# A hybrid decoder layer: DeltaNet rows in two buffers, mixer work moved between VectorE, GpSimd and ScalarE, and new task orders

## The chip, the cores and the metric

The kernel runs on one core of a Trainium2 chip. The metric is device time in microseconds of one launch. A core has TensorE (PE in the profile, its weight loads PEld), VectorE (DVE), ScalarE (ACT), GpSimd (POOL) and SyncE (SP), which here only issues DMAs; each engine works through its own queue in order.

## What is computed

One layer with 512 tokens of width 1024, float32 throughout:

```python
h = swiglu(rms_norm(x, g1), w_gate, w_up, w_down)            # width 2816
x = x + 0.5 * rms_norm(h, g1_post)
u = rms_norm(x, g_mix)                                        # u @ w_in feeds three mixers:
o_nsa = g0*compressed_attn + g1*selected_attn + g2*window_attn   # 8 heads of 64, T5 bias
dq, dk, dv = split(silu(causal_conv4(dn_qkv)))                # gated DeltaNet, 4 heads of 128
o_dn  = rms_norm(gated_delta_rule(l2(dq), l2(dk), dv, log_decay, beta), g) * silu(z)
o_mem = cross_attention(mem_q, rms_norm(mem))                 # 4 heads of 128, 256 memory tokens
merged = sum(sigmoid(u @ w_branch_gate)[b] * (o_b @ w_branch[b]) for b in (nsa, dn, mem))
x = x + rms_norm(merged @ w_out, g_post)
x = x + 0.5 * rms_norm(swiglu(rms_norm(x, g2), ...), g2_post)
```

The delta rule in its chunked form solves, for each head and chunk, a unit lower triangular system whose matrix is `beta_i * (k_i . k_j) * exp(gc_i - gc_j)` below the diagonal, `gc` being the running sum of the log decay.

## The kernel before

Float32 products are made of three products of split operands (`mm3`, L115, with the lines L117, L118, L119 of the profile): a weight block is loaded (`wraw`), cast on ScalarE (`whi`, L106) and its remainder taken on VectorE or, for a chosen share, on GpSimd (`wlo`, L109). A projection of the mixer is 24 such products of 128x512. A `wraw` buffer can be loaded again only when the remainder has been taken, and all weight loads go through SP's queue.

The launch is one long program, unrolled. In order: the first layer's first tiles (from 0 us), the rest of the first FFN as Strassen-like products of seven (L489, to about 232), its down product and norms (to about 365), the mixer's projections and the DeltaNet (365 to 600), the sparse attention (600 to 760), memory attention and the gated merge (760 to 900), the output product and norm (to about 980), and the second FFN.

What runs inside a stage is cut into tasks, a letter with digits, and lists in the dictionary `PRM` give their order (`tasks`, L1413). The order is a priority: a scheduler at build time takes the ready instruction of the highest priority for each engine, so tasks interleave. `off` gives a task a lead of so many places; `pool` says which share of its weight remainders goes to GpSimd (0 none, 1 all, 2 every second, 3 every third). On the chip each queue is then fixed.

First layer (`order_s`): `wFIC` loads and splits the weights of tile F, I = 0 gate or 1 up, half C; `t0K` transposes four blocks of the first 256 tokens (`feat`); `P0C`, `P1C` are the half products of tiles 0 and 1 (`half`); `y` and `x` load the rest of the input; `R`, `n` are norms; `F` finish tiles.

Mixer (`order`): `cHS` is projection and causal convolution of head H, part S (0 query, 1 key, 2 value; `dn_conv`, L886). `hHS` (`dn_head`, L905) transposes it, takes the squares on ScalarE (L924), a chain of small VectorE steps for the inverse root (L138 to L148), scales (`kn` or `qs`, L930) and transposes back (L937, `ptk`). `rH` (`dn_rows`, L941) loads two rows of scalars spread over all partitions (`rows`: the running log decay and beta) and makes `eg` and `dec` by exponentials. `lH` (`dn_lt`) makes the triangular matrix from `kbT`, the key transform times beta, and sends it to memory; `kH` (`dn_qk`) makes the query side. For a pair of heads `bI` (`dn_subst`, L987) reads the 16x16 diagonal blocks back and inverts them in 30 small VectorE steps (L1001, L1003, tile `Bi`) and sends them out and in again (`Dc`); `eI` (`dn_double`) expands them into four block diagonal matrices (L1021); `dIK` doubles the inverse block size, `sIN` runs the states over the four chunks and `oI` ends. `i` and `z` are projections with tokens as rows, `a` the scalars of the decay, `x`, `p`, `f` the compressed keys, `q` the attention queries.

Attention (`order2`): `S` are scores and softmax of one head and branch over four query blocks (`nsa_soft`; L1305 bias and minimum on VectorE, L1306 exponential on ScalarE, then scaling by `psc`, one letter for each query block, v VectorE or s ScalarE), `P` transposes and evicts the probabilities (`nsa_pt`, three evictions by `ptc`), `V` and `W` the products with the values, `M` merge tiles. `order4` is the merge with memory attention, `order3` the output product.

Of the kernel before, what the change touches and what calls it, by code (L numbers as in the profile page):

```python
# [10 lines left out]
F32 = mybir.dt.float32  # L11
# [4 lines left out]
OP = mybir.AluOpType  # L16
AX = mybir.AxisListType
P = 128
D = 1024
KT = 8  # L20
TB = 4
# [18 lines left out]
class Body:  # L40
    def __init__(self, ctx, tc, a, out, tap):
        self.tc, self.nc, self.a, self.out, self.tap = tc, tc.nc, a, out, tap
        pool = lambda name, **k: ctx.enter_context(tc.tile_pool(name=name, **k))
        self.sp = pool("sp", bufs=2)
        self.cp = pool("cp", bufs=1)
        self.ring, self.ringi = None, 0
        self.nload, self.pool_every = 0, 0
        self.tp = pool("tp", bufs=2)
        self.wp = pool("wp", bufs=1)
        self.wx, self.nx = None, 0  # L50
        self.ps = pool("ps", bufs=1, space=bass.MemoryType.PSUM)
        self.dr = pool("dr", bufs=1, space=bass.MemoryType.DRAM)
        nc = self.nc
        wm = self.tp.tile([P, 512], BF16, tag="tmpb", bufs=2, name="wm")
        nc.vector.memset(wm, 0.0)
        w1 = self.sp.tile([P, 1], F32, tag="w1", name="w1", bufs=1)
        nc.gpsimd.memset(w1, 0.0)
        nc.scalar.activation(w1, w1, AF.Silu)
        pw = self.bank("o", "warm")
        for _ in range(PRM.get("warm", 10)):  # L60
            nc.tensor.matmul(pw, wm[:, :P], wm, start=True, stop=True)
        self.cst = self.cp.tile([P, C_END], F32, name="cst")
        nc.sync.dma_start(self.cst[:, :P], a["consts"][:, :P])
        x = self.load_x(a["x"], tbs=(0, 1), c=slice(0, 512))
        self.ident = self.cst[:, C_ID : C_ID + P]
        self.gpre = self.sp.tile([P, 4, KT], F32, name="gpre", bufs=1)
        self.msk = self.sp.tile([P, 9], F32, name="msk", bufs=1)
        nc.sync.dma_start(self.gpre, a["gains_pre"])
        self.x0 = x
        self.own = 0  # L70
        self.side = []
# [869 lines left out]
    def dn_rows(self, h, sc, d):  # L941

        nc, g = self.nc, self.nc.gpsimd
        sg, gc, beta, nbg, dr = sc
        rows = self.da.tile([P, 2, TB, P], F32, tag="rows", name="rowsb", bufs=1)
        self.dma("r").dma_start(rows, dr[h].partition_broadcast(P))
        eg = self.da.tile(self.T4, F32, tag="eg", name="eg", bufs=1)
        dec = self.da.tile(self.T4, F32, tag="dec", name="dec", bufs=1)
        nc.scalar.activation(eg, rows[:, 0], AF.Exp)
        g.tensor_tensor(dec, rows[:, 0], gc[:, :, h, None].to_broadcast(self.T4), op=OP.subtract)  # L950
        g.tensor_tensor(dec, dec, self.cst[:, None, C_NEG : C_NEG + P].to_broadcast(self.T4), op=OP.add)
        nc.scalar.activation(dec, dec, AF.Exp)
        d.update(rows=rows, eg=eg, dec=dec)

    def dn_lt(self, h, d, dp):

        nc, v, g, te = self.nc, self.nc.vector, self.nc.gpsimd, self.nc.tensor
        kbT = self.da.tile(self.T4, F32, tag="kbT", name="kbT", bufs=1)
        g.tensor_tensor(kbT, d["kT"], d["rows"][:, 1], op=OP.mult)
        d["LT"] = dp.tile(self.T4, F32, tag="LT", name="LT", bufs=2)  # L960
        self.dn_kk(d["kT"], kbT, d["LT"], d["dec"])
        if h % 2 == 0:
            self.dL = self.dr.tile([2, TB, P * P + P], F32, name=f"dL{h}")
        self.dma("l").dma_start(self.dL[h % 2, :, : P * P].rearrange("n (p i) -> p n i", p=P), d["LT"])
        d["kd"] = dp.tile(self.T4, F32, tag="kd", name="kd", bufs=4)
        g.tensor_tensor(d["kd"], d["k"], d["dec"][:, :, P - 1 : P].to_broadcast(self.T4), op=OP.mult)

    def dn_qk(self, h, d, dp):

        g = self.nc.gpsimd  # L970
        d["qdT"] = dp.tile(self.T4, F32, tag="qdT", name="qdT", bufs=4)
        g.tensor_tensor(d["qdT"], d["qT"], d["eg"], op=OP.mult)
        d["gl"] = dp.tile([P, TB], F32, tag="gl", name="gl", bufs=4)
        g.tensor_copy(d["gl"], d["eg"][:, :, P - 1])
        d["QK"] = dp.tile(self.T4, F32, tag="QK", name="QK", bufs=4)
        self.dn_kk(d["kT"], d["qT"], d["QK"], d["dec"])

    def dn_kk(self, kT, rhs, dst, dec):
        p = self.psb("e", "pkk")
        for n in range(TB):  # L980
            self.nc.tensor.matmul(p[:, n], kT[:, n], rhs[:, n], start=True, stop=True)
        self.nc.vector.tensor_tensor(dst, p, dec, op=OP.mult)

    def dma(self, k):
        return getattr(self.nc, PRM.get("dma", {}).get(k, "sync"))

    def dn_subst(self, h, dp):  # L987

        nc, v, g = self.nc, self.nc.vector, self.nc.gpsimd
# [388 lines left out]
    def merge_tile(self, br, j, uh, ul, oh, ol, mg, first, gate=None, pair=None):  # L1378
        nc, v = self.nc, self.nc.vector
# [515 lines left out]
```

## Time and profile before

| | |
|---|---|
| median of three runs | 1285.19 us (1284.23 to 1287.13) |
| the profiled execution | 1285.44 us |
| its span, first to last instruction | 1283.7 us |
| mean granted TensorE clock | 0.994 |
| busy: TensorE, VectorE, ScalarE, GpSimd | 98%, 77%, 57%, 14% |
| chain that ended last | TensorE 84%, VectorE 8%, DMA 3%, ScalarE 3% |

The profile is one execution. Its page gives busy time by engine, the chain of work that ended last, and groups of instructions; further views give waits, stretches of time and single instructions. A matmul's end is modelled, so a busy TensorE can still run slowly: the granted clock has to be read beside it. A wait is put down to what came last before it ended. An idle engine that is not the bottleneck costs nothing.

### The profile page before, as it was taken

The page shows a single profiled execution, that of the slowest core. Times are in us where ns is not written, and L with a number is a line of the kernel's source. Part 1 is how long each engine was busy: PE and PEld are TensorE (multiplying, and loading weights), DVE is VectorE, ACT ScalarE, POOL GpSimd, SP SyncE. Part 2 cuts the span into 40 slices and gives each one's busy share as a digit, 9 for nine tenths or more (in the row PEclk, how much of TensorE's full clock was granted, in tenths as well). Part 3 has the DMA queues.
Part 4 walks back from the last instruction along what each step waited for, and adds up shares of the span by engine and source line. Part 5 has one row for each costly group of instructions (what it writes and reads, how often), then busy time and mean ns, then how long its engine had stood idle before and what let it go on. Part 6 is the DMA issues. An engine that isn't in the chain of part 4 may idle for free.

```text
span 1283.7 us, 21891 instructions
## 1 busy us (share of the span) xinstructions
PE 1258.7 (98%) x8067; PEld 1103.3 (86%) x8067; DVE 990.8 (77%) x1803; ACT 730.8 (57%) x1487; POOL 182.5 (14%) x208
## 2 busy tenths in 40 slices
PE   8999999999999999999999999999999999999997
PEld 7899999888787778888777778898888999998886
DVE  6897887598967866755789766675797987886888
ACT  6556665685755634415565545444676666655663
POOL 0011111130002221102221110010200121110300
PEclk9999999999999989999999999999999999999999
DMA  6567656894753341233221142131953677664963
GB/s 221 178 203 182 172 172 124 240 215 169 245 187 116 104 109 58 83 111 114 75 59 58 42 141 82 58 106 67 316 185 115 222 172 202 177 125 163 238 213 115
DMA packets 109243, 190.38 MB, mean 148 GB/s; under 512 B 18652, under 2 KB 28240, under 8 KB 109136
## 3 DMA queue, kind: packets, MB, share of 16 engines
q1 hardware_dynamic: 92976, 154.12, 36.5%
q0 software_dynamic: 15872, 34.61, 13.7%
q8 instruction: 63, 1.03, 0.3%
q10 hardware_dynamic: 288, 0.26, 0.1%
q14 instruction: 44, 0.36, 0.1%
HBM read 178.90 MB, written 33.08 MB: 165 GB/s over the span
## 4 chain that ended last, share of the span: by engine, by line
PE 84%; DVE 8%; DMA 3%; ACT 3%; issue 2%; SPq 0%; POOL 0%; DVEq 0%; ACTq 0%
PE smm L489 11%; PE se L489 7%; PE acc_mm L723 7%; PE pfm L117 5%; PE pfm L119 5%; PE pfm L118 5%; PE acc_s L723 4%; PE ss L489 4%; PE so L489 2%; PE sr L489 2%; PE ps L1303 2%; PE de L489 2%; PE po L1339 1%; PE ppt L1325 1%; PE acc_e L723 1%
## 5 line engine op out<-in xcount | busy, mean ns | idle before, releaser
L106 ACT CAST whi<-wraw 128x512 fp32r<-128x512 f32 (+1 forms) x174 | 105.5, 612 | 116.6 <-PE pfm L119 63.0
L109 DVE TENSOR_TENSOR wlo<-wraw,whi 128x512 fp32r<-128x512 f32 (+1 forms) x142 | 95.9, 684 | 36.7 <-ACT whi L106 35.2
L586 POOL DMA_DIRECT2D T<-in_ffn_d_dram x88 | 59.7, 678 | 377.8 <-PE pg L119 110.0
L117 PE MATMUL pfm<-xth,whi 128*128 128x512 f32 x272 | 107.9, 402 | 0.6 <-DVE X L1188 0.3
L118 PE MATMUL pfm<-xth,wlo 128*128 128x512 f32 x272 | 108.3, 403 | 0.0
L119 PE MATMUL pfm<-xtl,whi 128*128 128x512 f32 x272 | 107.8, 402 | 0.0
L489 PE MATMUL smm<-thi,fset 128*128 128x256 f32 x432 | 76.4, 277 | 0.5 <-ACT ss L496 0.5
L109 POOL TENSOR_TENSOR wlo<-wraw,whi 128x512 fp32r<-128x512 f32 x29 | 38.3, 1322 | 267.0 <-ACT whi L106 259.0
L489 PEld LDWEIGHTS smm<-thi,fset 128*128 128x128 f32 x432 | 65.2, 188 | 0.8 <-ACT ss L496 0.7
L117 PEld LDWEIGHTS pfm<-xth,whi 128*128 128x128 f32 x272 | 51.1, 189 | 10.9 <-issue 0.7
L119 PEld LDWEIGHTS pfm<-xtl,whi 128*128 128x128 f32 x272 | 50.9, 188 | 9.2 <-issue 0.4
L118 PEld LDWEIGHTS pfm<-xth,wlo 128*128 128x128 f32 x272 | 50.9, 188 | 8.7
L705 ACT CAST ringh<-ringr 128x1024 fp32r<-128x1024 f32 (+1 forms) x44 | 45.0, 1032 | 23.2 <-PE acc_mm L723 7.6
L489 PE MATMUL smm<-thi,fxth 128*128 128x256 f32 x204 | 56.4, 277 | 0.0
L489 PE MATMUL smm<-thi,fxtl 128*128 128x256 f32 x204 | 56.3, 276 | 0.0
L496 ACT COPY se<-smm 128x256 f32<-128x256 f32 x70 | 25.0, 358 | 53.4 <-PE smm L489 53.4
L489 PE MATMUL se<-thi,fset 128*128 128x256 f32 x288 | 50.8, 276 | 0.0
L738 DVE TENSOR_TENSOR sl<-H,sh 128x1024 fp32r<-128x1024 f32 (+2 forms) x38 | 40.9, 1080 | 5.4 <-ACT sh L737 5.3
L428 DVE TENSOR_TENSOR fs<-fq 128x1024 f32<-128x1024 f32 x35 | 43.3, 1238 | 1.0
L1306 ACT ACTIVATE Pm<-Pm,nm 128x384 f32<-128x384 f32 (+2 forms) x64 | 35.6, 557 | 14.4 <-DVE nm L1305 13.9
L489 PEld LDWEIGHTS se<-thi,fset 128*128 128x128 f32 x288 | 43.4, 188 | 0.0
L737 ACT CAST sh<-H 128x1024 fp32r<-128x1024 f32 (+2 forms) x38 | 35.4, 939 | 12.9 <-DVE H L645 4.1
(652 smaller groups left out, 4353.8 us busy)
## 6 DMA issues: line engine op xcount, KB each, us to landing
T<-in_ffn_d_dram POOLq DMA_DIRECT2D x88, 256.0 KB, 4.1
fq<-in_ffn_g_dram SPq DMA_DIRECT2D x70, 256.0 KB, 3.1
fq<-in_ffn_u_dram SPq DMA_DIRECT2D x70, 256.0 KB, 3.9
wraw<-in_ffn_d_dram SPq DMA_DIRECT2D x34, 256.0 KB, 3.7
ringr<-T SPq DMA_DIRECT2D x16, 512.0 KB, 5.7
ringr<-in_ffn_d_dram POOLq DMA_DIRECT2D x16, 512.0 KB, 8.1
woraw<-in_w_out_dram SPq DMA_DIRECT2D x32, 256.0 KB, 4.0
mfq<-in_w_gate_dram SPq DMA_DIRECT2D x28, 256.0 KB, 2.9
```

The costliest lines, as they stand in the source:

```text
L106: nc.scalar.copy(hi, raw)
L109: self.lmark = eng.tensor_tensor(lo, raw, hi.bitcast(F32), op=OP.subtract)
L117: t.matmul(out, lh, rh, start=first, stop=False)
L118: t.matmul(out, ll, rh, start=False, stop=False)
L119: self.tick(t.matmul(out, lh, rl, start=False, stop=last), 3 * math.prod(out.shape[1:]))
L428: add = lambda *x: v.tensor_tensor(*x, op=OP.add)
L489: m = lambda x, y, **kw: te.matmul(out, x, y, skip_group_check=True, **kw)
L586: i = g.dma_start(o[c], x[c], max_dma_last_dim=2048, **({"accum_op": OP.add} if add else {}))
L705: nc.scalar.copy(hi, raw)
L723: e = lambda a, b, s, f: nc.tensor.matmul(acc[i], a, b, start=s, stop=f, skip_group_check=True)
L738: last = tt(low, f, hi.bitcast(F32), op=OP.subtract)
L1306: nc.scalar.activation(pm, pm, AF.Exp, bias=nm[:, qb : qb + 1], scale=-1.0, accum_out=sm[:, qb : qb + 1])
```

## The change

- `rows` gets two buffers instead of one (another 4 KB of each partition).
- `dec` is made on VectorE in four operations of 128x128 (subtract, then add the mask) instead of two of 128x512 on GpSimd. `kbT` and the small `gl` move from GpSimd to VectorE; `kd` and `qdT` stay on GpSimd.
- The four block expansions of each pair (L1021) all go to GpSimd; three of four were on VectorE (`xpd`).
- Copies and scalings: the convolution's first scaling to ScalarE (`cva`), the scaling of the two narrow query blocks and the second eviction of the transposed probabilities to ScalarE (`psc`, `ptc`), the two copies of the third level swapped (`t1c`).
- In the first layer the gate half of tile 0's first half product goes first (`gu`), `t01` goes before `t00`, and a new task `m8` issues eight dummy products into an otherwise unused bank, the same as the eight at the start.
- New orders, leads and GpSimd shares for the first layer, mixer, attention, merge and output. `gon2` orders the last transposes of a pair behind the last scaled output. `mge` has the value it had.

```diff
-... 'xpd': (0, 1, 2), ... 'ptc': 'vvs', 'cva': 'v', ... 'psc': 'vvvv', ... 't1c': 'vs', ... 'gon2': 0}
+PRM = {'eng': {'rows': 2, 'dec': 's', 'dec2': 'v', 'kbT': 'v', 'kd': 'g', 'qdT': 'g', 'gl': 'v'}, ...
+... 'xpd': (), ... 'ptc': 'vss', 'cva': 's', ... 'psc': 'ssvv', ... 't1c': 'sv', ... 'gon2': 1, 'mge': 'v', 'gu': ((0, 1), (1, 0), (1, 0), (1, 0))}
 order_s (first layer), up to w111
-  w000 t00 w010 t01 P00 w110 y w100 t03 t02 P10 w011 w001 P01 w111
+  w000 t01 w010 t00 m8 w110 y P00 w100 t03 P10 t02 w011 w001 P01 w111
 order (mixer)
-  i a w c01 h01 r0 c00 c10 c02 l0 h00 h02 c11 c12 k0 h10 c22 h12 h11 c21 r1 k1 l1 h21 h22 b0 e0 z c20 r2 h20 c32 l2 c31
-  d00 k2 h31 r3 d01 l3 b1 d02 x0 s00 e1 d10 c30 h32 x1 h30 d11 s01 s02 s03 q3 p0 d12 o0 p1 k3 q0 p2 p3 s10 p4 q1 p5 s11
-  p6 p7 s12 s13 o1 q2 f
+  i a w c01 c10 h01 c00 r0 c02 l0 h00 h02 h10 c11 c12 k0 r1 h12 h11 c21 k1 c22 l1 b0 h21 h22 z c20 c32 e0 r2 h20 r3 c31 l2
+  d00 d01 h31 k2 l3 d02 x0 b1 h32 e1 s00 c30 s01 s02 s03 d10 x1 h30 d11 q3 p0 q0 d12 p1 o0 p2 p3 k3 s10 s11 p4 q1 p5
+  p6 s12 s13 p7 o1 f q2
 off (leads; those that the text names)
-  b0 300, h21 20, h22 100, e0 100
+  b0 100, h21 400, h22 20, e0 20
...
-        rows = self.da.tile([P, 2, TB, P], F32, tag="rows", name="rowsb", bufs=1)
+        rows = self.da.tile([P, 2, TB, P], F32, tag="rows", name="rowsb", bufs=PRM["eng"]["rows"])
...
-        g.tensor_tensor(dec, rows[:, 0], gc[:, :, h, None].to_broadcast(self.T4), op=OP.subtract)
-        g.tensor_tensor(dec, dec, self.cst[:, None, C_NEG : C_NEG + P].to_broadcast(self.T4), op=OP.add)
+        if PRM["eng"]["dec"] == "s":
+            for n in range(TB):
+                nc.vector.scalar_tensor_tensor(dec[:, n], rows[:, 0, n], gc[:, n, h : h + 1], self.cst[:, C_NEG : C_NEG + P], op0=OP.subtract, op1=OP.add)
...
-        g.tensor_tensor(kbT, d["kT"], d["rows"][:, 1], op=OP.mult)
+        self.eng("kbT").tensor_tensor(kbT, d["kT"], d["rows"][:, 1], op=OP.mult)
...
-                for i in (1, 0):
+                for i in PRM["gu"][2 * f + c]:
...
-                "w": weights, "P": half,
+                "w": weights, "P": half, "m": self.warm,
```

The new orders of attention, merge and output move single tasks by a few places: in attention the score task S001 goes behind P000, Q2 and Q3 go later, and the load of the memory keys (L) goes earlier; in the merge A00 goes first and A20 earlier; in the output stage the splits run 3 6 5 7 2 1 4 0 instead of 2 3 7 6 5 1 0 4.

More of the change, by code (lines that the diff above doesn't have):

```diff
@@ L59, in __init__, with warm @@
         pw = self.bank("o", "warm")
-        for _ in range(PRM.get("warm", 10)):
-            nc.tensor.matmul(pw, wm[:, :P], wm, start=True, stop=True)
+        def warm(n):
+            for _ in range(n):
+                nc.tensor.matmul(pw, wm[:, :P], wm, start=True, stop=True)
+        self.warm = warm
+        warm(PRM["warm"])
         self.cst = self.cp.tile([P, C_END], F32, name="cst")
@@ L949, in dn_rows @@
         nc.scalar.activation(eg, rows[:, 0], AF.Exp)
-        g.tensor_tensor(dec, rows[:, 0], gc[:, :, h, None].to_broadcast(self.T4), op=OP.subtract)
-        g.tensor_tensor(dec, dec, self.cst[:, None, C_NEG : C_NEG + P].to_broadcast(self.T4), op=OP.add)
+        if PRM["eng"]["dec"] == "s":
+            for n in range(TB):
+                nc.vector.scalar_tensor_tensor(dec[:, n], rows[:, 0, n], gc[:, n, h : h + 1], self.cst[:, C_NEG : C_NEG + P], op0=OP.subtract, op1=OP.add)
+        else:
+            self.eng("dec").tensor_tensor(dec, rows[:, 0], gc[:, :, h, None].to_broadcast(self.T4), op=OP.subtract)
+            self.eng("dec2").tensor_tensor(dec, dec, self.cst[:, None, C_NEG : C_NEG + P].to_broadcast(self.T4), op=OP.add)
         nc.scalar.activation(dec, dec, AF.Exp)
@@ L965, in dn_lt @@
         d["kd"] = dp.tile(self.T4, F32, tag="kd", name="kd", bufs=4)
-        g.tensor_tensor(d["kd"], d["k"], d["dec"][:, :, P - 1 : P].to_broadcast(self.T4), op=OP.mult)
+        self.eng("kd").tensor_tensor(d["kd"], d["k"], d["dec"][:, :, P - 1 : P].to_broadcast(self.T4), op=OP.mult)
     def dn_qk(self, h, d, dp):
@@ L971, in dn_qk @@
         d["qdT"] = dp.tile(self.T4, F32, tag="qdT", name="qdT", bufs=4)
-        g.tensor_tensor(d["qdT"], d["qT"], d["eg"], op=OP.mult)
+        self.eng("qdT").tensor_tensor(d["qdT"], d["qT"], d["eg"], op=OP.mult)
         d["gl"] = dp.tile([P, TB], F32, tag="gl", name="gl", bufs=4)
-        g.tensor_copy(d["gl"], d["eg"][:, :, P - 1])
+        self.eng("gl").tensor_copy(d["gl"], d["eg"][:, :, P - 1])
         d["QK"] = dp.tile(self.T4, F32, tag="QK", name="QK", bufs=4)
@@ L982, in dn_kk, with eng @@
         self.nc.vector.tensor_tensor(dst, p, dec, op=OP.mult)
+    def eng(self, k):
+        return self.nc.vector if PRM["eng"][k] == "v" else self.nc.gpsimd
     def dma(self, k):
@@ L1387, in merge_tile @@
         v.scalar_tensor_tensor(t2, t, 1.0, pp, op0=OP.add, op1=OP.mult)
-        return v.tensor_tensor(mg[:, j], mg[:, j], t2, op=OP.add)
+        return (nc.vector if PRM["mge"] == "v" else nc.gpsimd).tensor_tensor(mg[:, j], mg[:, j], t2, op=OP.add)
     def token_sums(self, k, uh, ul, tt, hi, lo):
```

2 lines of the change are left out of this document (1 added, 1 removed).

## The prediction

> **What bounds the kernel now.** I read the shares of the engines first, then busy time by stage, then the list of what TensorE waits for, then its clock, and only then single instructions.
>
> ```profile
> PE 1258.7 (98%) x8067; PEld 1103.3 (86%) x8067; DVE 990.8 (77%) x1803; ACT 730.8 (57%) x1487; POOL 182.5 (14%) x208
> ```
> ```profile
> 365.00:480.00 115.00, 107.30 (x564) 90.70 (x565) 80.68 (x198) 60.08 (x134) 22.56 (x23) 0.97 0.40 116
> 605.00:760.00 155.00, 153.95 (x834) 117.02 (x835) 124.94 (x344) 85.84 (x223) 25.70 (x20) 1.00 0.23 74
> 760.00:910.00 150.00, 148.92 (x939) 131.66 (x939) 98.31 (x145) 76.21 (x162) 14.35 (x10) 1.00 0.32 103
> ```
> ```profile
> core 0 of [0], span 1283.7 us
> engine line waited for: us in total, times, longest us
> PE ptk L937 <- DVE Bi L1003: 3.0, 1, 3.0
> PE pu L117 <- ACT k L466: 2.8, 1, 2.8
> PE ptk L937 <- DVE kn L930: 1.7, 1, 1.7
> PE warm L61 <- DVE wm L55: 1.2, 1, 1.2
> PE pfm L117 <- DVE tg L1387: 1.1, 1, 1.1
> PE acc_e L723 <- DVE wlo L109: 0.9, 1, 0.9
> PE ptk L937 <- DVE qs L930: 0.9, 1, 0.9
> PE ppt L1325 <- DVE Pm L229: 0.7, 1, 0.7
> PE pkk L981 <- POOL kbT L959: 0.7, 1, 0.7
> ```
>
> TensorE is busy 1258.7 of 1283.7 us, so 25.0 us of span is all that new orders can win by filling idle time. The columns of the stage rows are length, then busy time of PE, PEld, DVE, ACT and POOL. The mixer's first part (365 to 480) holds 7.7 us of the idle; attention (605 to 760) has 1.05 and the merge (760 to 910) 1.08. The wait list says where: four of the nine longest waits (3.0, 1.7, 0.9, 0.7) are the DeltaNet heads of the mixer, one (2.8) is the first layer. "Busy" hides a second loss, the clock:
>
> ```profile
> 6.33:9.18 2.85, 0.00 (x1) 0.00 (x1) 1.95 (x5) 2.03 (x5) 0.00 (x0) 1.00 0.87 308
> 9.44:12.85 3.41, 3.41 (x18) 3.41 (x18) 2.10 (x4) 1.19 (x3) 0.00 (x0) 0.50 0.74 249
> 456.58:460.00 3.42, 2.47 (x10) 2.40 (x11) 3.39 (x9) 0.49 (x1) 1.47 (x1) 0.50 0.22 69
> 460.00:463.41 3.41, 3.41 (x9) 2.64 (x9) 3.16 (x10) 0.71 (x2) 1.28 (x1) 0.50 0.16 49
> ```
>
> The value after the five engines is the granted clock. After the first layer's empty 2.85 us it is 0.50 for 3.41 us, all of them busy: half of that, 1.7 us, is lost on top of the gap. After the mixer's 3.0 us wait it is 0.50 for 2.47 + 3.41 = 5.88 busy us: 2.9 lost. So the two long waits cost 2.85 + 1.7 and 3.0 + 2.9. On what lowers the clock, the Trainium skill ("TensorE: Matmul & The Clock Gate", Part 1) states that it takes at least one idle window of about 3.4 us. The stretch of 3.41 us agrees; the idle of 2.85 before it does not, and the trace decides; what follows if the page is right stands among the rivals.
>
> **The change part by part.** First layer: the gate half of the first tile goes before the up half, two feature transposes are swapped, and eight dummy products follow them.
>
> ```profile
> 1.20 3.60 PE L61 MATMUL warm<-wm 128*128 128x512 bf16 x8 [1.20 <-DVE wm L55]
> ...
> 7.38 0.69 DVE L467 TENSOR_TENSOR k<-wraw,k 128x512 fp32r<-128x512 f32 x1
> ...
> 8.51 0.62 ACT L466 CAST k<-wraw 128x512 fp32r<-128x512 f32 x1 [0.78 <-DMA wraw<-in_ffn_u_dram]
> ...
> 13.92 0.84 ACT L212 ACTIVATE xth<-ptr,gpre 128x256 fp32r<-128x256 f32 x2 [2.18 <-PE ptr L208]
> ```
>
> The gate weights are split at 7.38 + 0.69 = 8.07, the up weights cast only at 9.13. With gate first TensorE can start 9.18 - 8.07 = 1.1 us sooner, and the dummies fill 6.33 to 8.1 and should keep the clock up: the same eight took 3.60 us before, 0.45 each, which is the pace of half clock (nine wide products in 3.41 us above, 0.38 each), so about 1.8 at full. At half clock they would run to 9.9 and cost 0.75. The most to be had is 2.85 + 1.7 = 4.55, the least a loss of 0.75. What is late next is the transfer of the next weights, whose buffers come free behind ScalarE's evictions; these stood idle 2.18 us for TensorE's transposes, and that is as far as they can move forward. I take -2.2. The dummies add no transfer and wait for nothing new.
>
> Mixer, the wait at 454 us. Its chain is in these rows (waits of SP's queue, waits of ScalarE, then single instructions):
>
> ```profile
> SPq L946 <- POOL kbT L959: 10.7, 3, 7.0
> ```
> ```profile
> ACT L949 <- DMA rowsb<-drows: 1.8, 1, 1.8
> ```
> ```profile
> 453.15 0.28 ACT L924 ACTIVATE sq<-ptr 128x128 bf16<-128x128 f32 x1
> ...
> 455.26 0.17 DVE L1001 TENSOR_TENSOR Bt<-Lb,Bi 64x15 f32<-64x15 f32 x1 [0.80 <-DMA Lb<-dL]
> ...
> 456.69 0.69 DVE L930 TENSOR_TENSOR kn<-ptr,dry 128x512 f32<-128x512 f32 x1
> 457.53 0.45 PE L937 MATMUL ptk<-cst,kn 128*128 128x128 f32 x1 [3.00 <-DVE Bi L1003]
> ```
>
> The one `rows` buffer is read last by kbT on GpSimd, so three of the four row loads held SP's queue, 10.7 us in all with the weight loads behind them. The load then lands late; ScalarE stands 1.8 us on it with a head's squares queued behind (last at 453.15); the head's norm on VectorE therefore meets the substitution, whose first step holds VectorE until its own transfer lands at 455.26; `kn` comes at 456.69 and TensorE has run out. A second buffer lets the row load go a head earlier: the 1.8 us go, the squares end near 451.6, and the small steps of the norm (L138 to L148) are through before the substitution's transfer blocks the queue. The order helps at the same place (the substitution's lead falls from 300 to 100, head 2's key transform gains one, from 20 to 400). I take the whole 3.0 + 2.9 = -5.9; the least is 0, if VectorE's queue still puts the substitution in front. Next in line is the substitution itself, which then starts no later than now.
>
> The 1.7 us wait for the first head's `kn`: one more projection (24 products) is placed ahead of that head. At full clock nine products take half of 3.41 us, so 24 take 4.5 and cover it: -1.7. The 0.9 wait for `qs` is merely moved: half, -0.45.
>
> Engines. The prices:
>
> ```profile
> L1021 DVE TENSOR_TENSOR Dm<-Dc,msk 128x512 f32<-128x512 f32 x4 | 3.8, 998 | 1.7 <-DMA Dc<-dD 1.7
> ...
> L1021 DVE TENSOR_TENSOR DT<-Dc,msk 128x512 f32<-128x512 f32 x2 | 1.4, 678 | 0.0
> ```
> ```profile
> L1021 POOL TENSOR_TENSOR DT<-Dc,msk 128x512 f32<-128x512 f32 x2 | 2.6, 1313 | 7.1 <-PE pfm L118 4.0 <-DMA Dc<-dD 3.2
> ```
> ```profile
> L951 POOL TENSOR_TENSOR dec<-dec,cst 128x512 f32<-128x512 f32 x4 | 5.1, 1283 | 0.3
> ```
> ```profile
> L229 DVE TENSOR_SCALAR cacc<-pfm,cw 128x512 f32<-128x512 f32 x12 | 9.0, 747 | 9.3 <-PE pfm L119 9.3
> ```
> ```profile
> L1306 ACT ACTIVATE Pm<-Pm,nm 128x512 f32<-128x512 f32 x16 | 11.5, 718 | 1.3 <-DVE nm L1305 0.9
> ```
>
> kbT on VectorE: 0.69 (the kn row, same size) for about 1.28, which takes 0.6 off the 0.7 wait: -0.6. Decay: two GpSimd passes of up to 1.28 a head become four VectorE passes over a quarter each; no row has that form, so 4 x 0.17 (the smallest VectorE step above) to 4 x 0.69 bounds them, 0.7 to 2.8 a head; nearer the first, a quarter of 0.69 being 0.17. Four heads of kbT and decay add 4 x (0.69 + 0.7) = 5.6 to VectorE; the conv's scaling to ScalarE takes 9.0 away, and three of the four expansions of each pair another 3.8 + 1.4 = 5.2. VectorE ends lighter by 8.6, behind TensorE and worth nothing by itself. The scaling waits on ScalarE for a projection's last product, as the VectorE row does now (9.3 us idle), and the casts of the next weights stand behind it; ScalarE is busy 60 of 115 us, so I give that nothing of its own.
>
> The expansions: four in a row on GpSimd take 4 x 1.31 = 5.2 us, where VectorE did three and GpSimd one side by side in about 3 x 1.0 = 3.0, so the level products can start 2.2 later per pair, 4.4 in all at worst. They are off the path where TensorE still has projections: from 365 to 480 it is short of operands, not of work. Behind them on GpSimd's queue stand the mask clears of the levels and the weight splits given to it, on whose buffers SP's loads wait. I take +0.5, ends 0 and +4.4. The Trainium skill ("GPSIMD Engine Reference", Specifications) speaks against this part: GpSimd shares its SBUF interfaces with VectorE and collides with its two-input operations. The trace agrees, 998 ns beside GpSimd and 678 without; were the eight VectorE operations beside each pair's expansions all stretched by that 0.32 us on the path, the time would be 5 us more, about 1282.
>
> Attention, merge, output. Scaling of the two narrow probability blocks and one eviction in three of the transposed ones go from VectorE (125 of 155 us busy) to ScalarE (86 of 155), and the orders move some tasks. Against me stand 16 blocks whose scaling now queues on ScalarE, for me the waits 0.7 (Pm) and 1.1 (tg). I take -1.0, ends -1.8 and the slow rival below. The order of the splits in the output stage, the swapped copies at the third level and the new shares of weight splitting on GpSimd I cost at nothing: TensorE's queue covers them, and where it doesn't they are new waits.
>
> New waits: an order that moves every head brings its own. The only row for that is the stretch itself: from 0 to another 7.7 us. I take 3.0, less than half, since VectorE is lighter.
>
> **Sum.** -2.2 - 5.9 - 1.7 - 0.45 - 0.6 + 0.5 - 1.0 + 3.0 = -8.35. The profiled execution took 1285.44 us (span 1283.7 and 1.7 around it), 0.25 above the median of 1285.19; so 1276.8, called 1277.
>
> **The rivals.** (a) The second buffer does not free the wait at 454, because VectorE's queue still holds the substitution in front of `kn`: +5.9, 1282.7. For it: the 0.80 us on the substitution's transfer stays. Against: the norm was late by ScalarE's 1.8 us first. (b) Waits only move: the mixer's new waits equal the old (7.7 of idle instead of 3.0 and the start held by transfers): 1276.8 + 4.7 + 2.2 = 1283.7, and without attention's 1.0, 1284.7. For it: every wait in the list is short and single, which is what a shuffled order leaves. (c) Idle time does not set the clock, so halves come where they came: 1276.8 + 2.9 = 1279.7, called 1280. This is where the clock page's window of 3.4 us would lead. Both half-clock stretches follow the longest waits, which speaks against it. (d) Slower: ScalarE as attention's queue. The scaling of a block there queues behind an exponential of the next (0.72 us), and the transposes wait for it, 16 times: 11.5 us, with attention's gain of 1.0 gone, 1289.3. It decides from about 0.6 us a block, 10 us together. Against: TensorE is full there (153.95 of 155) and has merge products to slip between.
>
> **How the numbers follow.** Forecast 0.60, (a) 0.12, (b) 0.10, (c) 0.04, (d) 0.14. 0.2% is 2.6 us, about what a measurement of this kernel can tell from no change. (a) lies on that edge, half of it to each side: faster 0.60 + 0.04 + 0.06 = 0.70; same 0.06 + 0.10 = 0.16; slower 0.14. The forecast's own range is 1269.5 (start -4.55, qs -0.9, attention -1.8, no new waits, no cost of expansions) to 1282. The range takes in (a), (b), (c) and the foot of (d): 1269 to 1287.
>
> **What would show it.** Right: TensorE's first product on weights near 8 us and no half clock before 13; no row wait of SP on kbT, no ScalarE wait on rowsb, no wait of ptk above 1 us and a clock of 1.00 through 480; the 365 to 480 work over 5 us shorter. Wrong: a new half-clock stretch anywhere, a wait of ppt on ScalarE in attention, pt waiting for GpSimd's expansions, or the start's gain given back to a weight transfer before 35 us.

## The result and the profile after

The changed kernel takes 1301.6 us in the median (1287.5 to 1303.3, 11 runs) against 1284.2 (1283.5 to 1287.1, 11 runs): ratio 1.0101, 95% interval 1.0073 to 1.0128. It is slower by 1%, where 1277 was forecast, with 1269 to 1287 as the range. The number needs one remark: the changed kernel's own times fall in two groups, 1287.5 to 1289.7 (4 runs) and 1299.8 to 1303.3 (7 runs). The profile below is of the quicker group (1287.5); one of the other group comes with the experiments.

The shares of the engines, the list of TensorE's waits, and the mixer's first part beside the two stretches where the clock had been at half before (columns as in the prediction: length, busy time of PE, PEld, DVE, ACT, POOL, granted clock, DMA share, GB/s):

```profile
PE 1261.5 (98%) x8075; PEld 1100.1 (86%) x8075; DVE 976.2 (76%) x1766; ACT 757.7 (59%) x1547; POOL 165.6 (13%) x193
```
```profile
PE pt L1055 <- DVE on L1116: 3.9, 1, 3.9
...
PE ptk L942 <- DVE kn L935: 0.8, 1, 0.8
```
```profile
365.00:480.00 115.00, 112.82 (x600) 94.87 (x600) 79.75 (x211) 67.86 (x154) 17.32 (x18) 1.00 0.41 122
9.44:12.85 3.41, 3.41 (x31) 3.41 (x31) 1.98 (x4) 1.76 (x5) 0.00 (x0) 1.00 0.86 281
456.58:463.41 6.83, 6.83 (x32) 5.66 (x31) 6.14 (x27) 2.96 (x4) 0.00 (x0) 1.00 0.29 101
```

Much of what was forecast is there. Both old stretches at half clock are at 1.00; the 3.0 us wait at 454 is gone, and the 1.7 us wait for `kn` is 0.8; the mixer's first part holds 600 product instructions in 115 us instead of 564. One sign is missing: SP's row loads still wait for `kbT`, 3.1 us instead of 10.7. But a new wait stands at the head of the list, longer than any before: the second pair's first level product (`pt`) waits 3.9 us for `on`, the output norm of the first pair. By the code, `pt` is written into the same two accumulator buffers (tag `s`) from which the norm still has to read. And the clock falls behind it:

```profile
537.19:540.60 3.41, 0.84 (x8) 0.87 (x8) 3.13 (x9) 0.00 (x0) 1.24 (x2) 1.00 0.13 52
540.60:544.02 3.42, 3.42 (x15) 3.03 (x13) 0.68 (x2) 0.62 (x1) 1.27 (x1) 0.50 0.00 0
544.02:547.43 3.41, 3.41 (x28) 2.96 (x27) 1.26 (x3) 0.00 (x0) 0.31 (x1) 1.00 0.21 77
```

Why `on` is late stands in single instructions of VectorE and of GpSimd in those microseconds (start, duration, engine, line, operation), and in the same steps in the kernel before, whose lines are five lower:

```profile
532.57 0.17 DVE L148 TENSOR_TENSOR dorz<-dorz,dorm 128x8 f32<-128x8 f32 x1
532.76 0.91 DVE L149 SCALAR_TENSOR_TENSOR dorz<-dorz 128x8 f32<-128x8 f32 x1
...
534.20 1.01 DVE L150 SCALAR_TENSOR_TENSOR dory<-dorz,dory 128x8 f32<-128x8 f32 x1
535.25 0.98 DVE L151 TENSOR_TENSOR dorz<-dory 128x8 f32<-128x8 f32 x1
536.26 0.97 DVE L152 SCALAR_TENSOR_TENSOR dorz<-dorz,dorm 128x8 f32<-128x8 f32 x1
537.27 1.19 DVE L153 SCALAR_TENSOR_TENSOR dory<-dorz,dory 128x8 f32<-128x8 f32 x1
```
```profile
532.58 2.61 POOL L1033 TENSOR_TENSOR Dm<-Dc,msk 128x512 f32<-128x512 f32 x2 [24.07 <-DMA Dc<-dD]
535.15 2.06 POOL L1033 TENSOR_TENSOR DT<-Dc,msk 128x512 f32<-128x512 f32 x2
537.18 1.25 POOL L981 TENSOR_TENSOR qdT<-qT,eg 128x512 f32<-128x512 f32 x1
```
```profile
544.32 0.17 DVE L144 SCALAR_TENSOR_TENSOR dorz<-dorz 128x8 f32<-128x8 f32 x1
...
545.12 0.17 DVE L148 SCALAR_TENSOR_TENSOR dory<-dorz,dory 128x8 f32<-128x8 f32 x1
```

Five steps of eight columns each take 0.91 to 1.19 us, 5.06 together, where the same five took 0.17 each, 0.85 together. The 4.2 us between are about the wait of 3.9. Beside them run, one after another, the four expansions, now all on GpSimd, and then `qdT`, which was there before too, and the ends match: each of the five ends 0.02 to 0.03 us behind one of GpSimd's operations. In the kernel before no operation of GpSimd ran beside these steps: `qdT` was over by 543.0.

So there were two theories at this point. A: the expansions on GpSimd hold VectorE's small steps back, hence the late `on`, the wait and the clock. O: the new order puts the second pair's products too close behind the first pair's norm, whatever the engine.

### The profile page after: what moved, and what is told of

It reads as the page before. It is cut to its first block, busy times and chain, and to the rows that moved or that the text cites. A ratio compares the mean times of both kernels' runs of the same rounds, so it can differ in the third digit from the quotient of the medians.

```text
span 1285.7 us, 21908 instructions
## 1 busy us (share of the span) xinstructions
PE 1261.5 (98%) x8075; PEld 1100.1 (86%) x8075; DVE 976.2 (76%) x1766; ACT 757.7 (59%) x1547; POOL 165.6 (13%) x193
## 4 chain that ended last, share of the span: by engine, by line
PE 85%; DVE 7%; DMA 3%; ACT 3%; issue 2%; SPq 0%; DVEq 0%; ACTq 0%
PE smm L494 11%; PE se L494 7%; PE acc_mm L728 7%; PE pfm L122 5%; PE pfm L123 5%; PE pfm L124 5%; PE acc_s L728 4%; PE ss L494 4%; PE de L494 2%; PE so L494 2%; PE sr L494 2%; PE ps L1315 2%; PE ppt L1337 1%; PE po L1351 1%; DVE wlo L114 1%
## 5 line engine op out<-in xcount | busy, mean ns | idle before, releaser
L114 DVE TENSOR_TENSOR wlo<-wraw,whi 128x512 fp32r<-128x512 f32 (+1 forms) x147 | 103.1, 711 | 38.4 <-ACT whi L111 36.4
L114 POOL TENSOR_TENSOR wlo<-wraw,whi 128x512 fp32r<-128x512 f32 (+1 forms) x24 | 30.8, 1283 | 280.1 <-ACT whi L111 267.5
L439 ACT CAST fset<-fq 128x512 fp32r<-128x512 f32 x54 | 33.6, 622 | 15.5 <-PE ss L494 14.4
```

Source lines behind the costliest of these rows:

```text
L114: self.lmark = eng.tensor_tensor(lo, raw, hi.bitcast(F32), op=OP.subtract)
```

## The experiments

**The changed kernel again**, three times unchanged, above all for a profile of the slower group.

> The changed kernel once more, unchanged; its times so far lie in two groups, 1287.5 to 1289.7 (clock 0.997) and 1299.8 to 1303.3 (clock 0.986). Clock 0.986 instead of 0.997 is about 0.011 x 1300 x 2 = 28 us more at half clock, and costs half of that, 14 us. Theory A (the wait sets it): in a profile of the slower group the half clock begins within a window of 3.4 us behind the 3.9 us wait of pt at 535.6 and lasts some 30 us. Theory B (small products alone): it begins elsewhere, in 480 to 505 or 545 to 570 us, with no wait of over 1 us ahead of it. If the profile is of the quicker group again it tells only how often the groups come.

> The changed kernel unchanged, for a profile of the slower of its two groups of times (1300 to 1303). Theory A (the wait sets the clock off): the half clock begins within 3.4 us behind the 4 us wait of pt near 536 and lasts about 28 to 35 us, through the stretch of 64-column products. Theory B (small products alone): it begins elsewhere with no wait over 1 us ahead. A time near 1289 tells nothing new.

> As again2, one more look for the slower group; the same expectations.

The first gave 1300.9 in the median of 9 runs (1289.6 to 1303.3), ratio 1.0096 (1.0064 to 1.0127): the groups again, 4 and 5 runs, and a profile of the quicker group (1289.6) with the wait and two windows at half clock behind it. The third, one execution of 1291.4, has the wait and one such window. The second, 1302.8, is of the slower group. Its windows of 3.41 us, from the wait on:

```profile
538.58:541.99 3.41, 0.00 (x0) 0.00 (x0) 3.31 (x7) 0.34 (x1) 2.13 (x2) 1.00 0.58 229
541.99:545.40 3.41, 3.16 (x12) 2.90 (x13) 1.56 (x6) 0.62 (x1) 0.00 (x0) 0.50 0.00 0
545.40:548.82 3.42, 3.42 (x17) 3.32 (x16) 0.42 (x1) 0.00 (x0) 1.27 (x1) 0.50 0.25 73
...
569.30:572.71 3.41, 3.41 (x9) 1.94 (x9) 0.42 (x1) 0.00 (x0) 0.00 (x0) 0.50 0.18 25
572.71:576.12 3.41, 3.41 (x26) 2.35 (x26) 0.00 (x0) 1.66 (x4) 0.00 (x0) 1.00 0.34 129
```

The wait is the same 3.9 us, but here the clock stays at 0.50 from 541.99 to 572.71, nine windows, 30.7 us, although TensorE counts as busy in all of it but 0.25 us at the start. Half of that is 15.4 us lost; with one window, as in the other profile, it is 1.7. The 13.7 between them are the distance of the two groups. What stands in these windows are the level products of 64 columns and the state products, one by one, with a wide product here and there; the last window, nine instructions in all, is mostly wide ones, and behind it the clock is full again. Right behind the wait stand short level products, then four wide products (`pfm`), then short ones again, in every profile of this kernel. What differs is where the windows cut them. The windows at half clock with `pfm` alone, in the profile of 1287.5, in that of 1289.6 (its second window) and in this one (here length, busy time of PE, PEld, DVE, ACT, then the clock):

```profile
540.60:544.02 3.42, 2.05 (x4) 1.21 (x4) 0.00 (x0) 0.00 (x0) 0.50 0.00 0
```
```profile
542.25:545.66 3.41, 1.78 (x4) 0.87 (x3) 0.00 (x0) 0.00 (x0) 0.50 0.00 0
```
```profile
541.99:545.40 3.41, 1.46 (x4) 1.21 (x4) 0.00 (x0) 0.00 (x0) 0.50 0.00 0
545.40:548.82 3.42, 0.59 (x2) 0.00 (x0) 0.00 (x0) 0.00 (x0) 0.50 0.25 73
```

Behind the windows with 2.05 and 1.78 us of wide products the clock is full; behind those with 1.46 and 0.59 it stays at half, though the last was busy throughout. Busy time does not order them: the first window of the profile of 1289.6 was busy for only 1.97 us, less than the 3.16 here, and half clock ended one window later. So the clock falls where the theory of the wait put it, and the two groups hang on where the windows cut the four wide products.

**Three expansions back on VectorE, both pairs.**

```diff
-'xpd': (),
+'xpd': (0, 1, 2),
```

> The changed kernel with three of the four expansions of each pair back on VectorE, nothing else. Theory A (four expansions in a row on GpSimd make VectorE's small operations slow, 1.0 us instead of 0.17, and so the norm ahead of the wait): the 3.9 us wait falls under 1.5 us, the half clock behind it goes, all times lie in one group near 1288 - 3.9 - 1.7 = 1282 to 1284. Rival O (the order puts the norm and its reader too close, whatever the engine): the wait stays at 2 to 4 us, the two groups stay, median near 1300. In both, VectorE is busy about 5 us more.

1287.9 (1285.9 to 1291.1), ratio 1.0025 (1.0015 to 1.0036), one group. The wait of `pt` fell to 0.4, so A. But the time is above the 1282 to 1284 expected, because a new wait came 60 us earlier, with one window at half clock behind it:

```profile
PE ptr L917 <- ACT cy L901: 3.1, 1, 3.1
```
```profile
472.23 2.16 DVE L1033 TENSOR_TENSOR Dm<-Dc,msk 128x512 f32<-128x512 f32 x2 [2.10 <-DMA Dc<-dD]
474.31 0.73 DVE L899 SCALAR_TENSOR_TENSOR cacc<-pfm,cw,cacc 128x509 f32<-128x509 f32 x1
```

In the changed order the first pair's expansions stand ahead of a convolution in VectorE's queue; VectorE stands 2.1 us on their transfer and works 2.2 us on them, and the convolution behind them is late. So for the first pair GpSimd was the right place, and only the second pair's expansions fall beside a norm.

**The order of before on the changed engines**, with all expansions on GpSimd, and then with three of the second pair's on VectorE:

```diff
-'order': [... 'c31','l2','d00','d01','h31','k2', ... 's00','c30','s01','s02','s03','d10', ...]
+'order': [... 'l2','c31','d00','k2','h31','r3', ... 's00','e1','d10','c30','h32','x1', ...]   # and off, pool of these tasks
...
-eng = v if 2 * w + i in PRM.get("xpd", (0,)) else g
+eng = v if 2 * w + i in ((0, 1, 2) if h else ()) else g      # second kernel only
```

> The changed kernel with the mixer's task order, leads and GpSimd shares of before; engines, second row buffer, first layer, attention and output as changed. Rival O (the new mixer order makes the wait): no wait of pt over 1 us, one group of times, 1281 to 1284. Theory A (GpSimd's expansions make it): the small operations of the norm still take about 1 us beside the expansions and a wait of 2 us or more stays at that place; times near 1287 or in two groups. It also tells whether the wait at 454 us goes with the second row buffer alone.

> The changed kernel with the whole mixer order of before (as order_b, 1287.3) and the second pair's expansions back on VectorE. If the expansions on GpSimd are the cause in either order: the 4.0 us wait of pt goes here too, the 2.6 us wait of ptk at 454 us stays, 1287.3 - 4.0 = 1283.3. If in this order the norm ahead is late for another reason: the wait stays at 2 us or more, 1286 to 1287.

The first: 1287.3 (1285.2 to 1291.7), ratio 1.0026 (1.0016 to 1.0037). Its waits:

```profile
PE pt L1055 <- DVE on L1116: 4.0, 1, 4.0
PE ptk L942 <- DVE Bt L1013: 2.6, 1, 2.6
```

The old order has the 4.0 us wait of `pt` as well, and in its profile five steps of the norm take 0.98 to 1.19 us beside the four expansions and a weight remainder on GpSimd; theory O falls as the cause of the wait. It does not have the upper group of times; half clock behind the wait lasts 10.2 us in its profile, which is of its slowest run. That the changed order adds the stretch of short products behind the wait, in which the clock stays down, fits this, but was not tested by itself. And the wait at 454 is still there with two row buffers, although SP's wait for `kbT` is down to 3.9 us and ScalarE no longer waits for the rows. The second: 1286.0 (1281.5 to 1290.5), ratio 1.0013 (0.9999 to 1.0027), waits 1.7 for `on` and 1.9 at 454: the wait on the norm shrinks but does not go, and the times spread by 9 us. In its profile VectorE's three expansions stand between the norm's steps (0.68 us each), and two steps take 1.04 and 1.25 us beside the expansion and a weight remainder left on GpSimd. The 1283.3 expected was missed; it supports A only in part.

**The first pair's expansions on GpSimd, three of the second pair's on VectorE**, in the changed order (the second edit above alone):

> The changed kernel with the expansions of the first pair of heads left on GpSimd and three of the four of the second pair back on VectorE. With all on GpSimd the second pair's made the 3.9 us wait of pt behind the norm; with both pairs back on VectorE that wait was gone, but the first pair's expansions (2.1 us of VectorE waiting for the transfer into Dc and 2.8 of work) stood in VectorE's queue ahead of a convolution and made a new wait of 3.1 us for cy, with one window at half clock. Theory A (both waits are queue effects of where the expansions stand): neither wait is over 1 us, one group of times at 1288.6 - 3.9 - 1.7 = 1283. Rival M (waits only move): another wait of 2 to 4 us takes their place, 1287.

1285.3 (1283.4 to 1286.7), ratio 1.0005 (0.9996 to 1.0015). Both waits are gone (`pt` 0.3, none above 1.3 in the list), its profile has no window at half clock before the end, and one group is left. This edit of one line takes 16 us from the changed kernel's median. It is 2 us above the 1283 expected, and no quicker than before.

**The second pair's expansions cut in four, still on GpSimd.** This leaves every queue's order as it is, and asks how GpSimd holds VectorE back.

```diff
-eng.tensor_tensor(X[i]..., Dc[:, w, i, :, None, :]..., bm, op=OP.mult)                       # 128x512
+[eng.tensor_tensor(X[i]...[:, n], Dc[:, w, i, n, None, :]..., bm[:, n], op=OP.mult) for n in four quarters]   # if h
```

> The changed kernel (1301, two groups) with each of the second pair's four expansions on GpSimd cut into four of 128 columns; every engine's order stays as it is. Theory L (GpSimd locks VectorE out for the length of one of its operations, so that VectorE's small operations get through one per GpSimd operation): five operations of the norm that took 0.9 to 1.2 us take about 0.3 to 0.4 each, 3 us sooner; the wait of pt falls from 3.9 to about 1 us, no half clock, one group of times near 1288.6 - 3 - 1.7 = 1284. Rival B (a share of bandwidth: the norm is slow as long as GpSimd is busy): the wait stays above 3 us and the two groups stay, median near 1300.

1284.7 (1281.7 to 1286.8), ratio 1.0004 (0.9995 to 1.0014), one group. VectorE's steps and GpSimd's operations:

```profile
534.78 0.39 DVE L148 TENSOR_TENSOR dorz<-dorz,dorm 128x8 f32<-128x8 f32 x1
535.21 0.33 DVE L149 SCALAR_TENSOR_TENSOR dorz<-dorz 128x8 f32<-128x8 f32 x1
...
537.17 0.33 DVE L153 SCALAR_TENSOR_TENSOR dory<-dorz,dory 128x8 f32<-128x8 f32 x1
```
```profile
534.75 3.45 POOL L1033 TENSOR_TENSOR Dm<-Dc,msk 128x128 f32<-128x128 f32 x8 [24.05 <-DMA Dc<-dD]
538.16 2.91 POOL L1033 TENSOR_TENSOR DT<-Dc,msk 128x128 f32<-128x128 f32 x8
```

The same work on the same engine, now 6.4 us long instead of 4.7, and yet the steps beside it take 0.33 to 0.39 instead of 0.91 to 1.19, and the wait of `pt` is 0.7. GpSimd is busy for longer and the norm is quicker: what counts is the length of one operation, as with a lock, and not a share of a bandwidth.

**The two mechanisms by themselves.**

> Nothing of the layer is computed; a kernel of its own. First part, TensorE: 70 wide products (512 columns); a pause of some 5 us; 160 short ones (64 columns, fp32) and then 30 wide; a pause; 60 wide; a pause; 30 wide, 160 short, 30 wide; a pause; 160 short, 30 wide. Theory A (a nearly empty stretch of 3.4 us halves the clock, only a stretch of wide products restores it, short ones do not lower it): half clock behind the first and last pause through all short products (160 x 0.21 = 34 us) and into the wide; behind the second pause 3.4 to 6.8 us; none in the third part after its first windows. Theory B (short products alone lower the clock): half clock in the third part too, within 7 us of the change to short ones. Second part, VectorE and GpSimd: ten operations of 128x8 beside six GpSimd products of 128x512, with two inputs and with one input, and ten of two inputs beside 24 GpSimd products of 128x128. Theory L (lock): with two inputs about 1.1 us each beside the long ones, 0.3 to 0.4 beside the short ones, 0.17 with one input. Theory B' (share): about the same slow-down beside long and short.

This is one execution of a kernel of its own. First TensorE. The runs of products (start, duration, and the pause ahead of them; a short product of 64 columns counts as two instructions), and the granted clock in the first and the third stretch of short ones:

```profile
27.00 68.53 PE L1910 MATMUL b<-w,L 128*128 128x64 f32 x320 [3.55 <-DVE w L1899]
95.29 8.40 PE L1906 MATMUL b<-r,Lr 128*128 128x512 f32 x30
...
136.49 35.84 PE L1910 MATMUL b<-w,L 128*128 128x64 f32 x320
```
```profile
27.00:95.00 68.00, 68.00 (x319) 68.00 (x319) 0.41 (x1) 0.00 (x0) 0.50 0.00 1
...
136.50:172.30 35.80, 35.80 (x322) 35.80 (x321) 0.00 (x0) 0.00 (x0) 1.00 0.00 1
```

The same 160 short products take 68.5 us behind a pause and 35.8 behind wide ones. They do not lower the clock, and they do not raise it again either, in 68 us of full business. The price of the pause is 32.7 us here, and only the wide products behind end it. The last part repeats it (68.0 us behind a pause of 3.55), and wide products alone behind a pause had one or two windows at half clock, as expected. Theory A for the clock holds, B falls. The wide products here are also of another type (`F32R` in the code, one instruction each). The type alone is not it: the half clock of 10.2 us in the old order ended behind a window with 3.2 us of 256-column products in plain float32. What else counts beside the width was not tested. Then VectorE and GpSimd: ten small operations, first eight alone, then beside GpSimd products of 512 columns (two inputs, one input), then beside ones of 128 columns:

```profile
261.70 1.56 DVE L1923 TENSOR_TENSOR s<-s,w 128x8 f32<-128x8 f32 x8
...
265.46 6.73 DVE L1923 TENSOR_TENSOR s<-s,w 128x8 f32<-128x8 f32 x10
...
274.27 6.74 DVE L1924 TENSOR_SCALAR s<-s 128x8 f32<-128x8 f32 x10
...
283.08 3.81 DVE L1923 TENSOR_TENSOR s<-s,w 128x8 f32<-128x8 f32 x10
```
```profile
265.51 8.00 POOL L1933 TENSOR_TENSOR m<-m,w 128x512 f32<-128x512 f32 x6 [265.07 <-DVE m L1930]
...
283.12 9.91 POOL L1935 TENSOR_TENSOR m<-m,w 128x128 f32<-128x128 f32 x24 [0.80 <-DVE m L1930]
```

Alone a step takes 1.56 / 8 = 0.20 us; beside the long operations (8.00 / 6 = 1.33 each) 0.67, two to each of them; beside the short ones (9.91 / 24 = 0.41 each) 0.38, about one to each. The pace follows the length of GpSimd's single operation, as a lock's would. Two expectations missed: not 1.1 but 0.67 in the mean, since every second step slips in as one operation of GpSimd ends and the next begins and takes 0.17, while the others take 1.11 to 1.13 and end 0.02 us behind GpSimd's; and the steps with one input, expected at 0.17, are held as much as those with two.

**The first layer alone**, on the kernel before, and **the dummies alone** taken out (of the kernel of 1285.3):

```diff
-'order_s': ['w000','t00','w010','t01','P00', ...]
+'order_s': ['w000','t01','w010','t00','m8','w110','y','P00', ...]   # with offs, gu of the change; all else as before
...
-'t00','m8','w110'
+'t00','w110'                                                        # second kernel
```

> The kernel before with the first layer of the changed one alone (gate half first, transposes swapped, eight dummy products, the new leads). If the 2.7 us won by 230 us lasts: 1284.2 - 2.7 = 1281.5. If it only moves into later waits: 1284, with the end of the first layer 2.7 us earlier but the end of the mixer where it was.

> As xpd_mix (1285.3), without the eight dummy products between the first weights, the gate half still first. If the dummies hold the clock through the start: without them TensorE is empty 1.5 to 2 us near 6.5 to 8.5, a window at half clock comes in 8 to 13, and the time is 1.7 us longer, 1287. If the gap is short enough without them: 1285 or a little less, no half clock.

The first: 1283.5 (1281.3 to 1286.8), ratio 0.9997 (0.9987 to 1.0006), not to be told from no change, where 1281.5 was expected. The second: 1284.9 (1283.7 to 1285.5), ratio 1.0003 (0.9994 to 1.0011), also equal to the kernel with them. Their profiles do show the clock fall in a window with 1.90 of 3.42 us busy when the dummies are out, but it fell in a kernel that has them as well, the next one, with 1.91 us busy:

```profile
7.01:10.43 3.42, 1.90 (x8) 1.12 (x7) 2.79 (x6) 2.90 (x7) 0.00 (x0) 1.00 0.86 305
10.43:13.84 3.41, 3.41 (x18) 3.41 (x18) 1.39 (x3) 0.48 (x1) 0.00 (x0) 0.50 0.80 240
```

**One row buffer** instead of two; otherwise the kernel of 1285.3.

```diff
-'eng': {'rows': 2,
+'eng': {'rows': 1,
```

> As xpd_mix (1285.3), with one buffer of rows instead of two and nothing else. If the second buffer is what freed the wait at 454 us, as predicted: the three row loads hold the queue again for some 10 us, a wait of ptk of about 3 us comes back, 1288 to 1289 with a window at half clock in part of the runs. If the order alone freed it: 1285, no wait of ptk above 1.2 us.

1288.6 (1287.6 to 1289.4, 5 runs), ratio 1.0034 (1.0022 to 1.0046): the buffer is worth 3 to 4 us in the changed order. Not by one wait of 3 us, though; the wait at 454 came back as 0.7, beside a `kn` of 1.5, 1.3 for `zg` and 1.1 for a weight. With the order of before and two buffers the wait at 454 was 2.6: for this wait the order does most, and the buffer's 3 to 4 us lie in several small ones. The row loads, expected to hold SP's queue for some 10 us again, wait 3.8 us for `kbT` and 2.4 for the substitution.

**Attention, merge, output and the memory's stage as before** (orders, leads, `psc`, `ptc`), on the kernel of 1285.3:

```diff
-'order2', 'order3', 'order4' and their off, pool of the change;  'psc': 'ssvv', 'ptc': 'vss'
+those of before;                                                 'psc': 'vvvv', 'ptc': 'vvs'
```

> As the one before it, and besides with attention, merge, output and the memory's stage as before: their orders, leads, GpSimd shares, the block scalings and the evictions of transposed blocks on VectorE. If these parts brought the 1.0 us predicted, it is slower than the one before it by 1.0. If they lost what the profiles show between the mixer's end and the last product (688.2 us against 686.8 before), it is quicker by about 1.4. Equal within 1 us: the parts are worth nothing either way.

1286.0 (1284.9 to 1288.2), ratio 1.0018 (1.0009 to 1.0028) against 1.0005: slower by some 0.7 to 1.7 us, with intervals that touch. The parts seem to bring about the 1.0 that was forecast; it is not settled.

**The order of before from the first level product on**, the changed order up to there; then the same with all four of the second pair's expansions on VectorE and a longer lead for the norm:

```diff
-'order': [... 'c31','l2','d00','d01','h31','k2', ...]   'off': {... 'o0': 50, 'e1': 200}
+'order': [... 'c31','l2','d00','k2','h31','d01', ...]   'off': {... 'o0': 400, 'e1': 100}   # first
+                                                        'off': {... 'o0': 600, 'e1': 0}     # second, and eng = v if h else g
```

> The changed kernel with the first pair's expansions on GpSimd and three of the second pair's on VectorE (as in xpd_mix, 1285.3), and with the mixer's order, leads and GpSimd shares of before from the first level product on; up to there the changed order. In xpd_mix the waits of the mixer are gone and yet the stretch from the first projection of the mixer to the compression's last products takes 231.3 us, against 230.7 with the order of before and 3.5 us more of waits: the level products begin 4.3 us sooner and the states end 1.5 us later. Theory P (the changed order of the tail packs the short products together and TensorE pays for it between them): the tail of before on the changed head wins about 4 us: 1281. Rival Q (the tail is long because its operands come when they come, whatever the order): 1285, with waits of 2 us or more back in the tail.

> As hybrid (1282.6, profile with a 1.6 us wait of pt on the norm and 10 us at half clock behind it), with all four expansions of the second pair on VectorE, the norm's lead raised (400 to 600) and that of the expansions lowered (100 to 0). If the wait left is the expansions between and beside the norm's steps: it falls under 0.7 us, no half clock, 1282.6 - 1 to - 3 = 1280 to 1281.5. If VectorE's added work (0.7 us) and the order only shift it: 1282 to 1283.

The first: 1282.6 (1279.5 to 1286.9), ratio 0.9992 (0.9980 to 1.0005), with 10.2 us at half clock behind a `pt` wait of 1.6 in its profile. The second: 1281.9 (1280.4 to 1284.5), ratio 0.9983 (0.9972 to 0.9995), `pt` 1.1. It is quicker than the kernel before by 0.17%, and so quicker than both; the wait left on the norm was expected under 0.7, and the time under 1281.5. In its profile the four expansions still stand between the norm's first steps, and one step takes 1.28 us beside a weight remainder on GpSimd. Why the tail of the order counts shows in the stretch from the mixer's first product to the first score on the compressed keys (`pcl`), which holds the same products in every kernel: in the one with the first layer alone changed (order of before), the one of 1285.3 (changed order) and this one, all at full clock (columns as in the prediction):

```profile
368.52:599.22 230.70, 223.21 (x1334) 186.98 (x1333) 150.58 (x407) 102.12 (x248) 43.19 (x48) 1.00 0.33 98
```
```profile
369.02:600.33 231.31, 227.47 (x1335) 187.61 (x1334) 147.76 (x413) 107.76 (x258) 31.31 (x37) 1.00 0.34 98
```
```profile
369.20:598.15 228.95, 223.67 (x1335) 186.89 (x1333) 146.26 (x414) 107.56 (x258) 30.74 (x36) 1.00 0.34 99
```

The changed order leaves TensorE idle for 3.8 us instead of 7.5, but the same products keep it busy for 4.3 us longer; with the tail of before it is idle for 5.3 and busy for 0.5 longer. The largest single part of the 4.3 lies in the compression's products (64 instructions), which stand among the level and state products, in the same three kernels:

```profile
L1214 PE MATMUL phid<-w,X 128*64 128x256 f32 x64 | 8.5, 390 | 0.0
```
```profile
L1214 PE MATMUL phid<-w,X 128*64 128x256 f32 x64 | 11.0, 393 | 0.5 <-DMA w<-in_cmp_w_dram 0.5
```
```profile
L1214 PE MATMUL phid<-w,X 128*64 128x256 f32 x64 | 9.1, 390 | 1.0 <-DMA w<-in_cmp_w_dram 1.0
```

The mean of one is the same, 0.39 us, but they overlap each other less: 2.5 us more of busy time where the changed order puts them singly between others. Some of that lies under their neighbours; counted from each start to the next it is 2.0.

## Why the prediction was wrong

One term of the sum was wrong in kind, and the others were worth less than thought. With that term left out, 1276.3 was forecast, and the kernel with its cause taken away for the second pair takes 1285.3: the other terms promised some 9 us that did not come. That 1285.3 lies in the range is no credit to them.

The step that failed is "the expansions: +0.5, ends 0 and +4.4". With that one line undone for the second pair the ratio falls from 1.0101 to 1.0005, with its operations cut in four to 1.0004: the term measured some 12 us by the ratios (0.0096 x 1284), 16 by the medians and 2 to 4 in the quicker group. The prediction priced four expansions in a row by their own length, by what waits for them (the level products) and by what stands behind them on GpSimd's queue. It did not ask what runs on VectorE beside them. The sentence drawn from the Trainium skill ("GPSIMD Engine Reference", Specifications: GpSimd shares its SBUF interfaces with VectorE) pointed at this; the prediction stretched eight large operations by 0.32 us each, "about 1282". The trace agrees with the page on the collision, but where it cost time was the chain of small operations, which lost 0.8 us a step. On the list of what would make the forecast wrong stood "a new half-clock stretch anywhere" and "`pt` waiting for GpSimd's expansions"; both came, the second by way of the norm.

The second failure is the price of half clock. The prediction took what the trace of before showed, that one or two windows follow a wait, and so lost 1.7 to 2.9 us. How long it lasts depends on what stands behind the wait, up to 30.7 us here. The rival that idle time does not set the clock falls: the two profiles and the experiment by itself show the pause ahead of it. What the Trainium skill states ("TensorE: Matmul & The Clock Gate", Part 1), that a busy window of about 3.4 us brings the clock back, does not hold here if busy is what the profile calls so: seven windows in the changed kernel and nineteen in each of two parts of the small one were busy throughout and did not.

The other terms:
- Start, -2.2: the half clock is gone in the changed kernel's profile, but alone the part measures -0.4 by its ratio, with an interval of -1.7 to +0.8, and the dummies nothing.
- Wait at 454 and its clock, -5.9: gone, but not by the step that was to do it. With the buffer, the changed engines and the order of before, SP's long wait and ScalarE's wait for the rows go as forecast, and the wait stays at 2.6 us for `Bt`, the substitution, which is rival (a); with the changed order and one buffer it is 0.7. So the late rows alone did not make it; the order, which sets the substitution's place in VectorE's queue, did most. And the clock part was no fixed cost: with a wait of 2.6 us too, and 1.67 us of products in its window where the kernel before had 1.36, the kernel with the first layer alone had full clock there,

```profile
456.00:464.00 8.00, 8.00 (x38) 6.62 (x37) 7.35 (x26) 1.84 (x3) 1.83 (x2) 1.00 0.46 131
```

  so 2.9 us of the gain had been read from one execution.
- `kn` -1.7 and kbT -0.6: 0.8 of 1.7 stayed; the kbT wait is gone, at 0.69 us an operation as taken from the `kn` row. The decay's quarters were not near 0.17 but 0.34 each, 1.4 us a head, within the bounds; one that began beside GpSimd took 1.20.
- Attention -1.0: about that, not settled. Rival (d) did not come; TensorE's longest wait on the scaling there is 0.6 us, against 0.7 before.
- New waits, +3.0: with both big ones repaired the list holds none above 1.3, and still nothing is won. The time is then that of rival (b), 1284.7, but the waits have not moved; they have gone. The mixer's stretch measured above takes 231.3 us with 3.8 of idle, and with the order of before and all its waits 230.7.

This is the loss that the sum had no term for: what the changed order saves in idle time (3.7 us) it pays in busy time (4.3). Products of projections used up early to fill the head's waits are missing in the tail; that the short products which then stand alone there are the whole of the 4.3 is not shown. With the tail of before on the changed head the stretch is 228.9 us, and that is the kernel of 1281.9.

Two small slips in the working change nothing: the lower end adds up to 1269.7 and not 1269.5; and nine products in 3.41 us counted those that the window's edges cut, and at full clock they start 0.23 us apart in the profiles, so that 24 take 5.4 us and not 4.5.

## What to carry to other kernels

When work moves to GpSimd, look not only at what waits for it but at what runs on VectorE at the same moment: a chain of tiny steps is hurt by the length of GpSimd's single operations, so cut them, or put them where no chain runs. Price a new wait of about 3 us on TensorE by what stands behind it: here wide products ended a half clock within a window or two, short ones did not. And a wait filled with work taken from later is only won if the later stretch can spare it: look at the busy time of the whole stretch, and not at its waits alone.

## What the runs showed of the hardware that was not expected

- A GpSimd operation on 128x512 made 128x8 steps of VectorE last until its own end, 0.91 to 1.19 us instead of 0.17; operations of a quarter, 0.33 to 0.39. One-input steps were held alike (0.67 us in the mean, with or without a second input).
- The clock's fall and its return have different conditions. In the layer's profiles every window of 3.41 us (cut where the clock can change) with 0 to 1.4 us of products was followed by half clock; of those with 1.6 to 2.0 some were (1.90, 1.91) and some were not (1.67 at 454 with the first layer alone changed). And 35.8 us of 64-column products without a pause kept it at 1.00, and the same products kept it at 0.50 for 68 us behind a pause of 3.55 us.
- The same wait of 3.9 us cost 1.7 or 15.4 us more, and what differed was how the windows cut the four wide products behind it: 1.78 and 2.05 us of them in one window ended half clock, 1.46 did not. Where the threshold lies, and whether it is one of width alone, was not tested.
